# Diagonal score blocks of an HGRN2 recurrence as two alternating 64-column products

## The chip, the core and the metric

The kernel runs on one core of one Trainium2 chip. The metric is the device time of one execution in microseconds (us); lower is better. Three executions of the kernel before took 622.64, 622.67 and 622.85 us, a median of 622.67 us. Inputs and outputs are float32.

## The reference, cut to what matters

One decoder layer with model width 1024 over 512 tokens: a gated linear recurrence (HGRN2, 8 heads of 128) and a latent attention (8 heads) run side by side, are gated, merged, and added to the residual stream. The change concerns only the scores inside the recurrence. It is computed in chunks of 32 tokens:

```python
b = jnp.cumsum(log_f, axis=3)
q_in = q * jnp.exp(b)
k_in = k * jnp.exp(-b)
k_out = k * jnp.exp(b_last - b)
scores = jnp.einsum('nbhtk,nbhsk->nbhts', q_in, k_in)
scores = jnp.where(causal, scores, 0.0)
o_intra = jnp.einsum('nbhts,nbhsv->nbhtv', scores, v)
# between chunks: state = state * decay + k_out^T v ; o_inter = q_in . state
```

## The kernel before, in words

The kernel is one long stream of products on TensorE, fed by weights that arrive by DMA. Most products are the projections of the 512 tokens with the weight matrices. Each float32 weight is split on the chip into a high part (a ScalarE cast, line 113) and a low part (a VectorE subtraction, line 114), and a projection is three products (lines 90, 91 and 92, in helper `mm3`).

The recurrence is done for pairs of heads (`hg_pair`, called for pairs 0 to 2 in the loop at line 716 and for the last pair at line 733). A pair projects the forget gate and works out running products of it (`hg_forget`), projects values, queries and gate, builds the states at the ends of 128-token tiles (`hg_states`), and then computes scores (`hg_scores`), outputs (`hg_out`) and gated results (`hg_gate`). The kernel does not use chunks of 32 on their own: it joins four chunks into a tile of 128 tokens and carries a state only between tiles. So each head has NT = 4 diagonal score blocks of 128 keys by 128 queries, and the pairs of chunks inside such a block need differently scaled operands. `hg_scores` therefore writes a block in three layers, one over the other, into one PSUM tile `aps` per head:

- line 511: `ki` times `qi`, the whole 128x128 block. Right on the four 32x32 chunk diagonals; elsewhere it is written over or masked.
- line 517: `ko` times `qi`, 32x32 blocks for chunk 0 to chunk 1 (PSUM partitions 0 to 31) and chunk 2 to chunk 3 (partitions 64 to 95). Its loop runs over the two chunk positions outside and the four tiles inside.
- line 522: `k64` times `q64`, a 64x64 block for the first two chunks to the last two.

In the words of the change, products that start at PSUM partition 0 and products that start at partition 64 belong to different column groups of TensorE; a product's number of output partitions is its number of weight columns (the profile writes 128*32 for 128 rows and 32 columns). `C` is 32, `P` is 128. All three layers are plain float32 products, each of which shows in the trace as two weight loads and two matmuls: line 511 makes 16 matmuls for a pair of heads, line 517 makes 32, line 522 makes 16.

Line 523 is one VectorE instruction per head, a predicated copy: where `mask_le` (key not after query) is set, it copies the PSUM tile to `asb` in SBUF. `asb` is set to zero once at the start (line 434), so masked places stay zero. `hg_out` then multiplies `asb` with the values (line 533) and adds the part from the states (line 535); ScalarE squares the result (line 539), GpSimd works out the root of the mean (lines 160 and 161), VectorE scales (line 541), and TensorE turns the result around (line 549).

The order on each engine comes from the framework's planner, which simulates the program from its own costs (`schedule_with_timeline_sim=True`, line 1145), so for pairs 0 to 2 nobody has written out where the score products stand among the projections. For the last pair, TensorE's order is written out by hand (`manual_schedule`, line 726): scores, then a gate projection inside which the outputs are placed, then the first attention scores. PSUM tiles come from two pools: 3 banks for projections (`mm`) and 5 for everything else (`ax`).

Of the kernel before, what the change touches and what calls it, by code (L numbers as in the profile page):

```python
# [18 lines left out]
P = 128  # L19
D = 1024  # L20
S = 512
NT = S // P
# [16 lines left out]
def hybrid_layer(ctx: ExitStack, tc: tile.TileContext, a):  # L39
    nc = tc.nc  # L40
# [15 lines left out]
    def ax_tile():  # L56
        return ax.tile([P, 512], F32, tag="ax", name="ax_ps")
# [301 lines left out]
    mask_le = const.tile([P, P], U8, name="mask_le")  # L359
# [70 lines left out]
    for i in range(2):  # L430
        gh = hw.tile([P, NT, 12], F32, f"gh{i}")
        nc.gpsimd.memset(gh[:], 1.0)
        asb = hw.tile([P, S], F32, f"asb{i}")
# [71 lines left out]
    def hg_scores(heads):  # L505

        res = [(asb_[h % 2], ax_tile()) + t for h, t in heads]
        for _, aps, ki, ko, k64, qi, q64 in res:
            for i in range(NT):
                b = slice(i * P, i * P + P)  # L510
                nc.tensor.matmul(aps[:, b], ki[:, b], qi[:, b], start=True, stop=True)  # L511

        for _, aps, ki, ko, k64, qi, q64 in res:
            for c in (0, 2):
                for i in range(NT):
                    blk = lambda n: slice(i * P + n * C, i * P + n * C + C)
                    nc.tensor.matmul(aps[c * C : c * C + C, blk(c + 1)], ko[:, blk(c)], qi[:, blk(c + 1)],
                                     start=True, stop=True)
        for asb, aps, ki, ko, k64, qi, q64 in res:
            for i in range(NT):  # L520
                b = slice(i * 64, i * 64 + 64)
                nc.tensor.matmul(aps[0:64, i * P + 64 : i * P + P], k64[:, b], q64[:, b], start=True, stop=True)
            nc.vector.copy_predicated(asb[:].rearrange("p (g t) -> p g t", g=NT),
                                      mask_le[:].rearrange("p (o t) -> p o t", o=1).broadcast_to([P, NT, P]),
                                      aps[:].rearrange("p (g t) -> p g t", g=NT))
        return [r[0] for r in res]

    def hg_out(h, asb, st_, q128, v_sb):
# [30 lines left out]
    def hg_pair(pair, before_gate=None, last=None):  # L559
# [23 lines left out]
        def scores():  # L583
            return hg_scores([(h, kk[i][2:5] + qq[i][0:2]) for i, h in enumerate(hs)])
# [121 lines left out]
    def gates(b, c, hook=None, to=None):  # L706

        res = []
        for i, ps in enumerate(proj_ch(w_in, COL_G + b * D + c * 256, hT, hook)):
            j = 8 * b + 2 * c + i  # L710
            g = z_tile()[:] if to is None else to[:, 2 * c + i]
            nc.scalar.activation(g, ps[:], AF.Tanh, scale=0.5, bias=hb_gate[:, j : j + 1])
            res.append(g)
        return res
# [130 lines left out]
    g = first_gates  # L845
    for c in range(1, 4):
        g = g + gates(0, c, to=ma)
# [41 lines left out]
    part = {}  # L889
# [259 lines left out]
```

## Time and profile before

| | |
|---|---|
| median of three executions | 622.67 us |
| span of the profiled execution (first to last instruction) | 620.6 us |
| TensorE busy (PE) | 610.0 us, 98% |
| weight loads (PEld) | 521.3 us, 84% |
| VectorE busy (DVE) | 397.4 us, 64% |
| ScalarE busy (ACT) | 260.2 us, 42% |
| GpSimd busy (POOL) | 117.9 us, 19% |
| matmuls of line 511 / 517 / 522 | 64 / 128 / 64 |

The span runs from the first to the last instruction. The profile gives no separate total for the profiled execution; the 2.07 us between its span and the median lie outside the instructions. A matmul's duration in the trace covers its way through the array, and matmuls follow each other before the one ahead has ended; so a rate is read from the starts of neighbours, not from durations.

### The profile page before, as it was taken

The numbers are of one execution on the slowest core, as the hardware profiler recorded it, in microseconds if no ns is written. First come the engines' busy times: TensorE is split into PE (matmuls) and PEld (weight loads), VectorE is DVE, ScalarE is ACT, GpSimd is POOL, SyncE is SP. The second block draws the span as 40 slices with busy tenths as digits, with TensorE's granted clock in tenths as the row PEclk, the third lists the DMA queues.
The fourth block names the chain that finished last, engine by engine and source line by source line (L and its number), as shares of the span: only waits on it lengthen the run. The fifth ranks groups of instructions, "written<-read, shape, count | busy, mean of one in ns | idle before, by whom it ended". The sixth has DMA issues, their size and how long they took to land.

```text
span 620.6 us, 8808 instructions
## 1 busy us (share of the span) xinstructions
PE 610.0 (98%) x3336; PEld 521.3 (84%) x3336; DVE 397.4 (64%) x625; ACT 260.2 (42%) x483; POOL 117.9 (19%) x219
## 2 busy tenths in 40 slices
PE   8999999999999999999999999999999999999995
PEld 4998888888888888888888888888899988888884
DVE  7727855398864539847667767738257842447895
ACT  5645243323144231445445555444354532334352
POOL 3106300231320033231414123001210012000011
PEclk9999999999999999999999999999999999999998
DMA  7425153223205202423223232329942899600403
GB/s 248 143 67 175 63 145 92 69 69 101 69 2 170 80 22 56 118 53 106 74 70 101 56 87 85 101 69 326 248 123 56 268 356 288 200 0 1 169 1 135
DMA packets 62377, 72.35 MB, mean 117 GB/s; under 512 B 6104, under 2 KB 48510, under 8 KB 62336
## 3 DMA queue, kind: packets, MB, share of 16 engines
q1 hardware_dynamic: 58476, 61.37, 31.9%
q0 software_dynamic: 2160, 7.87, 6.3%
q10 hardware_dynamic: 1700, 2.56, 1.4%
q8 instruction: 26, 0.43, 0.3%
q14 instruction: 15, 0.12, 0.1%
HBM read 60.25 MB, written 2.10 MB: 100 GB/s over the span
## 4 chain that ended last, share of the span: by engine, by line
PE 96%; DVE 2%; ACT 1%; DMA 0%; issue 0%; POOL 0%; POOLq 0%; ACTq 0%; DVEq 0%
PE mm_ps L90 23%; PE mm_ps L92 23%; PE mm_ps L91 23%; PE ax_ps L875 6%; PE ax_ps L983 4%; PE ax_ps L672 2%; PE mm_ps L266 2%; PE ax_ps L693 1%; PE ax_ps L511 1%; PE ax_ps L533 1%; PE ax_ps L92 1%; PE ax_ps L91 1%; PE ax_ps L90 1%; PE mm_ps L875 1%; PE mm_ps L983 1%; PE ax_ps L535 1%
## 5 line engine op out<-in xcount | busy, mean ns | idle before, releaser
L114 DVE TENSOR_TENSOR w_lo<-w_raw,w_hi 128x1024 fp32r<-128x1024 f32 (+3 forms) x86 | 102.5, 1195 | 97.4 <-ACT w_hi L113 96.5
L90 PE MATMUL mm_ps<-hT,w_hi 128*128 128x512 f32 x384 | 150.9, 393 | 0.0
L91 PE MATMUL mm_ps<-hT,w_hi 128*128 128x512 f32 x384 | 150.0, 391 | 0.0
L92 PE MATMUL mm_ps<-hT,w_lo 128*128 128x512 f32 x384 | 149.8, 392 | 0.0
L113 ACT CAST w_hi<-w_raw 128x1024 fp32r<-128x1024 f32 (+3 forms) x86 | 85.1, 992 | 143.6 <-PE mm_ps L91 83.9
L92 PEld LDWEIGHTS mm_ps<-hT,w_lo 128*128 128x128 f32 x384 | 72.1, 188 | 14.6
L91 PEld LDWEIGHTS mm_ps<-hT,w_hi 128*128 128x128 f32 x384 | 72.2, 188 | 14.4
L90 PEld LDWEIGHTS mm_ps<-hT,w_hi 128*128 128x128 f32 x384 | 72.2, 188 | 14.3
L92 PE MATMUL mm_ps<-w_hi,hT 128*128 128x512 f32 (+1 forms) x96 | 36.7, 384 | 0.0
L91 PE MATMUL mm_ps<-w_lo,hT 128*128 128x512 f32 (+1 forms) x96 | 36.5, 382 | 0.0
L90 PE MATMUL mm_ps<-w_hi,hT 128*128 128x512 f32 (+1 forms) x96 | 36.4, 386 | 0.0
L680 POOL TENSOR_SCALAR p<-p,sm 128x128 f32<-128x128 f32 (+3 forms) x28 | 16.9, 606 | 64.1 <-DVE sm L679 37.8
L455 DVE RECIPROCAL tf<-pr 128x512 f32<-128x512 f32 x8 | 26.8, 3351 | 0.2
L678 ACT ACTIVATE p<-ax_ps,sm 128x128 f32<-128x128 f32 (+3 forms) x32 | 16.9, 530 | 23.6 <-DVE sm L677 21.1
L90 PE MATMUL mm_ps<-yb,w_hi 128*128 128x512 f32 x64 | 24.9, 389 | 0.0
L91 PE MATMUL mm_ps<-yb,w_hi 128*128 128x512 f32 x64 | 24.9, 389 | 0.0
L92 PE MATMUL mm_ps<-yb,w_lo 128*128 128x512 f32 x64 | 24.9, 389 | 0.0
L541 DVE TENSOR_TENSOR k<-ax_ps,ss 128x512 f32<-128x512 f32 x8 | 5.5, 692 | 24.7 <-POOL ss L161 24.7
L156 DVE TENSOR_TENSOR pt<-ax_ps,pt 128x512 fp32r<-128x512 f32 (+1 forms) x24 | 13.6, 593 | 11.3 <-ACT pt L155 11.3
L90 PE MATMUL mm_ps<-cT,w_hi 128*128 128x512 f32 x52 | 20.8, 400 | 0.0
L92 PEld LDWEIGHTS mm_ps<-w_hi,hT 128*128 128x128 f32 x96 | 18.0, 188 | 3.0
L91 PEld LDWEIGHTS mm_ps<-w_lo,hT 128*128 128x128 f32 x96 | 18.0, 188 | 2.9
(284 smaller groups left out, 1172.8 us busy)
## 6 DMA issues: line engine op xcount, KB each, us to landing
w_raw<-w_in SPq DMA_DIRECT2D x58, 512.0 KB, 3.8
x<-w_proj_a SPq DMA_DIRECT2D x10, 512.0 KB, 6.5
x<-x POOLq DMA_DIRECT2D x8, 512.0 KB, 9.6
w_raw<-w_proj_b SPq DMA_DIRECT2D x8, 512.0 KB, 9.3
w_raw<-w_proj_a SPq DMA_DIRECT2D x4, 512.0 KB, 11.4
ya<-w_out SPq DMA_DIRECT2D x4, 512.0 KB, 7.4
t<-w_out SPq DMA_DIRECT2D x4, 512.0 KB
yb<-w_out SPq DMA_DIRECT2D x4, 512.0 KB, 9.5
```

Source lines behind the costliest of these rows:

```text
L90: nc.tensor.matmul(ps, lh[lsl], rh[rsl], start=start, stop=False)
L91: nc.tensor.matmul(ps, lh[lsl], rl[rsl], start=False, stop=False)
L92: nc.tensor.matmul(ps, ll[lsl], rh[rsl], start=False, stop=stop)
L113: nc.scalar.copy(hi[:, :o], raw[:, :o])
L114: (lo_eng or nc.vector).tensor_tensor(lo[:, :o], raw[:, :o], hi[:, :o].bitcast(F32), op=ALU.subtract)
L156: nc.vector.tensor_tensor(lo, src, hi.bitcast(F32), op=ALU.subtract)
L266: nc.tensor.matmul(ps, hT[l][:, 4 * kh + k, t * P : t * P + P], c_hl[kh][r][:, k * 256 : k * 256 + 256], start=kh == 0 and kind == 0 and k ...
L455: nc.vector.reciprocal(rp[:], pr[:])
L678: nc.scalar.activation(p[:, :n], sps[:, :n], AF.Exp, scale=SCALE, bias=sm[:, 1:2], accum_out=sm[:, 2:3])
L680: (nc.vector if final else nc.gpsimd).tensor_scalar(p[:, :n], p[:, :n], sm[:, 3:4], 0.5, op0=ALU.mult, op1=ALU.mult)
L875: nc.tensor.matmul(ps[:, o], w[k // 2][i][:, k % 2, cols], ap[j][:, k], start=not banks and c == 0 and n == 0, stop=n == 11, skip_group_ch ...
L983: nc.tensor.matmul(ps[:, o : o + n], ap[i][:, k, t * P : t * P + P], w[k // 2][j][:, k % 2, o : o + n], start=fresh and c == 0, stop=c == ...
```

## The change

Three edits, all in `hg_scores`. The 128x128 product becomes two products of 64 keys by 64 queries, one at PSUM partitions 0 to 63 (columns 0 to 63 of the block) and one at partitions 64 to 127 (columns 64 to 127), alternating. The loops around the 32-column products are exchanged, so that the two column groups alternate with each product. The lower left 64x64 quarter of the block is no longer written, so the predicated copy becomes two: partitions 0 to 63 with all 128 columns of each tile, partitions 64 to 127 with the last 64.

```diff
             for i in range(NT):
-                b = slice(i * P, i * P + P)
-                nc.tensor.matmul(aps[:, b], ki[:, b], qi[:, b], start=True, stop=True)
+                for n in range(2):
+                    b = slice(i * P + n * 64, i * P + n * 64 + 64)
+                    nc.tensor.matmul(aps[n * 64 : n * 64 + 64, b], ki[:, b], qi[:, b], start=True, stop=True)
 
         for _, aps, ki, ko, k64, qi, q64 in res:
-            for c in (0, 2):
-                for i in range(NT):
+            for i in range(NT):
+                for c in (0, 2):
                     blk = lambda n: slice(i * P + n * C, i * P + n * C + C)
...
-            nc.vector.copy_predicated(asb[:].rearrange("p (g t) -> p g t", g=NT),
-                                      mask_le[:].rearrange("p (o t) -> p o t", o=1).broadcast_to([P, NT, P]),
-                                      aps[:].rearrange("p (g t) -> p g t", g=NT))
+            for n in range(2):
+                part, cols = slice(n * 64, n * 64 + 64), slice(n * 64, P)
+                view = lambda t: t[part].rearrange("p (g t) -> p g t", g=NT)[:, :, cols]
+                nc.vector.copy_predicated(view(asb), mask_le[part, cols].rearrange("p (o t) -> p o t", o=1)
+                                          .broadcast_to([64, NT, P - n * 64]), view(aps))
```

## The prediction

> **What bounds the kernel now.** I read the spans and clock first, then the windows, then the timeline around the scores.
>
> ```profile
> core 0: 620.6 us, clock 0.996
> ```
> ```profile
> core 0: us, PE busy (x) PEld busy (x) DVE busy (x) ACT busy (x) POOL busy (x), PEclk, DMA share, GB/s
> 0.00:18.00 18.00, 14.84 (x80) 9.27 (x80) 13.65 (x28) 9.73 (x19) 6.84 (x19) 1.00 0.80 269
> 18.00:613.20 595.20, 595.13 (x3257) 512.03 (x3257) 381.94 (x593) 248.62 (x460) 109.63 (x198) 1.00 0.39 112
> 613.20:620.60 7.40, 0.00 (x0) 0.00 (x0) 1.80 (x4) 1.85 (x4) 1.44 (x4) 0.63 0.37 142
> ```
>
> The middle row decides: from 18 us to TensorE's last matmul at about 613.2 us, TensorE has a matmul in flight for 595.13 of 595.20 us, at full clock. Nothing keeps it waiting long enough to empty it. A busy TensorE can still be a slow one, so the question is how densely its matmuls follow each other inside the scores. The chain of waits agrees on whose time counts:
>
> ```profile
> PE 96%; DVE 2%; ACT 1%; DMA 0%; issue 0%; POOL 0%; POOLq 0%; ACTq 0%; DVEq 0%
> ```
>
> So time taken off TensorE's stream comes off the end, as long as no other engine then makes TensorE wait. The scores of one pair of heads, in the timeline of TensorE (start, us from first start to last end, line, shape, count):
>
> ```profile
> 105.39 0.39 PE L92 MATMUL mm_ps<-hT,w_lo 128*128 128x512 f32 x1
> 105.62 1.95 PE L511 MATMUL ax_ps<-qi,ki 128*128 128x128 f32 x16
> 107.50 0.90 PE L517 MATMUL ax_ps<-qi,ko 128*32 128x32 f32 x32
> 108.33 1.15 PE L522 MATMUL ax_ps<-q,k 128*64 128x64 f32 x16
> 109.40 0.50 PE L90 MATMUL mm_ps<-hT,w_hi 128*128 128x512 f32 x1
> 109.74 0.39 PE L91 MATMUL mm_ps<-hT,w_hi 128*128 128x512 f32 x1
> ```
>
> The kernel has four such stages, one for each pair: 64 matmuls of line 511 are 4 x 16.
>
> ```profile
> L511 PE MATMUL ax_ps<-qi,ki 128*128 128x128 f32 x64 | 7.8, 275 | 0.0
> L517 PE MATMUL ax_ps<-qi,ko 128*32 128x32 f32 x128 | 3.6, 199 | 0.0
> L522 PE MATMUL ax_ps<-q,k 128*64 128x64 f32 x64 | 4.6, 225 | 0.0
> ```
>
> **How fast each width runs.** A narrower window of the timeline leaves out the first matmuls of a run:
>
> ```profile
> 105.73 1.84 PE L511 MATMUL ax_ps<-qi,ki 128*128 128x128 f32 x15
> 108.49 0.98 PE L522 MATMUL ax_ps<-q,k 128*64 128x64 f32 x14
> ```
>
> Taking off the last one's own duration: (1.84 - 0.275) / 14 = 112 ns from one 128-column matmul to the next, and (0.98 - 0.225) / 13 = 58 ns for 64 columns. Half the width, half the time, with 4 to 5 ns that stay; the line through both gives 31 ns for 32 columns. If 64-column products came strictly one after another, twice as many of them would gain nothing: 2 x 58 = 116 against 112. All hangs on whether two column groups run at once.
>
> Line 517 shows that they can. Its 32 matmuls take (0.90 - 0.199) / 31 = 22.6 ns each, below the 31 ns of one after another, though its loop changes the column group only three times in a stage. Windows on line 517 show where:
>
> ```profile
> 107.49:107.65 0.16, 0.15 (x5) 0.15 (x6) 1.00 0.00 0
> 107.80:107.95 0.15, 0.15 (x17) 0.15 (x12) 1.00 0.00 0
> ```
>
> A window counts what begins in it and what is still in flight. In the first 0.16 us there is one group alone and 5 matmuls. In the later window 17 are seen; one group alone, at 31 ns with 199 ns in flight, would show (150 + 199) / 31 = 11. So near a change of group the next group's matmuls start while the last ones of the group before are still waiting their turn: two streams side by side. The count comes to (150 + 199) / 17 = 20.5 ns per matmul.
>
> **The change, part by part.** *The diagonal blocks.* A stage now has 32 matmuls of 64 columns, two (one product) for one half, two for the other. If the halves run side by side, each half takes 16 x 58 = 0.93 us. I add 0.03 us for the second half's later start (half a step, an estimate). Changing the width costs something: the last matmul of line 511 starts at 105.73 + 14 x 0.112 = 107.30, its turn is over at 107.41, and line 517 starts at 107.50, 0.09 us later. Of line 522, the first two steps take 108.49 - 108.33 = 0.16 us instead of 2 x 0.058 = 0.12, another 0.04 to 0.05. Before, line 511 had the same width as the projections ahead of it and paid neither; now it pays 0.14 us. From its first turn to the start of line 517: before 107.50 - 105.62 = 1.88 us; after 0.14 + 0.93 + 0.03 + 0.09 = 1.19 us. That is -0.69 us a stage. If the halves don't overlap at all, it is 0.14 + 32 x 0.058 + 0.09 = 2.09, or +0.21 us. These are the ends; I take the overlap, since the nearest row, line 517, shows it for the same data type, operand rows and PSUM tile.
>
> *The 32-column products.* Before, 108.33 - 107.50 = 0.83 us, of which 0.09 is the change of width after them and about 0.02 the slow first step. With groups alternating throughout: 16 x 0.031 + 0.02 + 0.02 + 0.09 = 0.63 us, or -0.20. If the 20.5 ns counted above is all that can be issued, 32 x 0.0205 + 0.11 = 0.77, or -0.06. I take -0.15.
>
> *Line 522 and what follows it* stay as they are, the 0.11 us (109.74 - 109.40 against 0.23 of a usual projection step) that the return to full width costs included.
>
> *The predicated copy.* One instruction per head becomes two. Half the partitions is no cheaper, as line 626 shows beside line 523; half the elements is:
>
> ```profile
> L523 DVE COPY_PREDICATED asb<-mask_le,ax_ps 128x512 f32<-128x512 uint8 x8 | 5.4, 728 | 1.2 <-PE ax_ps L522 1.2
> L626 DVE TENSOR_TENSOR qp<-qs,qh 64x512 fp32r<-64x512 f32 x8 | 5.8, 721 | 5.1 <-ACT qh L622 4.9
> L156 DVE TENSOR_TENSOR pt<-ax_ps,pt 128x256 fp32r<-128x256 f32 x8 | 3.3, 414 | 0.0
> ```
>
> So 0.73 us plus about 0.42 (between half of 0.73 and 0.46), 0.42 us more for each head, 0.84 us for each stage, 3.4 us over the kernel, all on VectorE. What hides it is the projection work that TensorE does between the scores and the outputs. In the stage where VectorE is most crowded:
>
> ```profile
> 164.82 1.35 DVE L523 COPY_PREDICATED asb<-mask_le,ax_ps 128x512 f32<-128x512 uint8 x2
> 169.71 0.60 PE L533 MATMUL ax_ps<-v,asb 128*128 128x128 f32 x4
> ```
>
> The copies end at 166.17 and TensorE wants `asb` at 169.71, 3.54 us later. If VectorE ends 0.84 us later and TensorE comes 0.84 us earlier, 1.9 us are left. Queued behind the copies on VectorE are the forget gates' steps and weight splits of the next pair; 0.84 us is little against the 381.94 busy of 595.20 us above.
>
> What is late next is the turn of the outputs, line 549, which needs VectorE's line 541:
>
> ```profile
> 122.00 0.69 DVE L541 TENSOR_TENSOR k<-ax_ps,ss 128x512 f32<-128x512 f32 x1 [1.19 <-POOL ss L161]
> 123.33 0.60 PE L549 MATMUL ax_ps<-ident,k 128*128 128x128 f32 x4
> ```
>
> Here only 123.33 - 122.69 = 0.64 us are spare. But that chain (squares, root, scaling) begins with TensorE's own outputs, so it moves ahead with TensorE; it would hurt only as far as it stands still, at worst 0.84 - 0.64 = 0.2 us in a stage, which I keep as the end of the range and take as nothing.
>
> *Sum.* -0.69 - 0.15 = -0.84 us a stage, x 4 = -3.4 us. The span goes from 620.6 to 617.2; outside it lie 622.67 - 620.6 = 2.07 us that the edit doesn't touch. Forecast: 622.67 - 3.4 = 619.3 us. Ends for this case: at most -1.0 a stage (no late start, cheap changes of width), 618.6; at least -0.75 a stage with 0.2 given back, 4 x 0.55 = 2.2, 620.5.
>
> **Where the Trainium skill speaks against it.** "TensorE: Matmul & The Clock Gate", Part 3, section "The mechanism", says that a weight load runs beside earlier matmuls only if its row group differs, and that matmuls start and end strictly in program order. All products here use all 128 rows, so by that rule alternating columns would gain nothing. Line 517 disagrees at 32 columns (17 matmuls where 11 would fit). "TensorEngine Tiling (Array Packing)", section "Key Properties", says instead that different tiles load and multiply in parallel, 128x64 having two; no run here yet shows it at 64.
>
> **Rivals.** *No overlap at 64 columns* (the change doesn't do what it says for the larger part): +0.21 from line 511 and -0.15 from line 517 make +0.06 us a stage, +0.2 us in all: 622.9 us, no change that can be measured. For it: the only 64-column rows in the profile, line 522, use a single column group. Against it: line 517. If line 517 loses its gain too, it is 4 x 0.21 = 0.84 us, 623.5 us, still within what can't be told. Chance of both 0.08. The first page's rule, taken at its word, ends at 623.5 us.
>
> *Half an overlap*, where loads share a path: two halves at 44 instead of 29 ns per matmul cost 32 x 0.015 = 0.48 us a stage more than forecast; 621.2 us. Chance 0.06.
>
> *Each change of column group costs what a change of width costs*, 0.09 us. Line 511 would make 15 such changes in a stage and line 517 15 instead of 3. With the serial +0.21, that is 0.21 + 27 x 0.09 = 2.6 us a stage, 10.6 us, 633.3 us: clearly slower. The point from which it decides lies at (0.31 - 0.21) / 27 = 4 ns per change, above which the result is slower by over 1.25 us. Against it: line 517's changes of group are where it is fastest. Chance 0.02.
>
> *The planner sets another order* for pairs 0 to 2, because its costs changed, and TensorE gets a wait or some more changes of width at 0.09 to 0.11 us. Nothing in the profile speaks for it except that the order there isn't written out. It would take twelve of them to eat 1.2 us; 620.0 to 623. Chance 0.04.
>
> **How the numbers follow.** A measurement of this kernel can tell about 0.2%, 1.25 us, from no change, so faster means below 621.4 and slower above 623.9. The forecast has 0.80. Faster: 0.80, most of the half overlap and a part of the planner, 0.86. Same: no overlap and the rest, 0.11. Slower: 0.03. The range reaches from 618.4, a little under the forecast's own lower end, to 621.2, which takes in the half overlap; no overlap and changes that cost stay out.
>
> **What would show it.** Right: line 511 (its new line) with 128 matmuls of 64 columns, 32 of them in a stage in about (0.14 + 0.96) us plus a duration of 0.22; line 517's 32 in about 0.7 us from first start to last end; line 523 with 16 instructions, two forms, about 0.73 and 0.42 us; TensorE still busy without a break from 18 us to its last matmul, which ends near 609.8 us. Wrong: 64-column matmuls of that line 58 ns apart on average (no overlap); a row of waits of TensorE for `asb` or for line 541; projections with another order ahead of the scores.

## The result and the profile after

The changed kernel takes 619.08 us (median of five executions, 618.88 to 619.32) against 622.67 us before (622.48 to 622.85). The ratio is 0.9943, with a 95% interval from 0.9931 to 0.9955: 3.6 us, 0.6%, faster.

The windows of the changed kernel, with the same columns as before (the end of TensorE's work has moved to 610.1 us):

```profile
18.00:610.10 592.10, 592.00 (x3323) 508.66 (x3321) 385.03 (x601) 248.93 (x460) 109.76 (x198) 1.00 0.39 112
610.10:617.60 7.50, 0.00 (x0) 0.00 (x0) 1.80 (x4) 1.85 (x4) 1.47 (x4) 0.72 0.36 140
```

TensorE still has a matmul in flight for all but 0.1 us of the stretch. It does 66 more matmuls in it (64 from the change, two at the window's edges), in 3.1 us less. VectorE works 3.1 us more. The last window, behind TensorE, is about as long as before (7.50 and 7.40 us). So the time came out of TensorE's stream, and the timeline of the first score stage shows where:

```profile
105.54 0.39 PE L92 MATMUL mm_ps<-hT,w_lo 128*128 128x512 f32 x1
105.86 1.15 PE L512 MATMUL ax_ps<-qi,ki 128*64 128x64 f32 x32
106.94 0.70 PE L518 MATMUL ax_ps<-qi,ko 128*32 128x32 f32 x32
107.57 1.15 PE L523 MATMUL ax_ps<-q,k 128*64 128x64 f32 x16
108.64 0.50 PE L90 MATMUL mm_ps<-hT,w_hi 128*128 128x512 f32 x1
108.98 0.39 PE L91 MATMUL mm_ps<-hT,w_hi 128*128 128x512 f32 x1
```

Read from the last projection ahead of the scores to the second one behind them, this is 108.98 - 105.54 = 3.44 us, against 109.74 - 105.39 = 4.35 us before. The first stage lost 0.91 us. The other three, read the same way from the matmul ahead of the scores, lost 0.91 us each as well (4.23 to 3.33 us). Four times 0.91 makes 3.64 us, and 3.59 were measured. The 32 matmuls of the new halves take as long from first start to last end (1.15 us) as the 16 equally wide ones of line 523 below them. That is what two streams side by side look like.

The copies became two kinds, one as dear as before, one cheaper:

```profile
L527 DVE COPY_PREDICATED asb<-mask_le,ax_ps 64x512 f32<-64x512 uint8 x8 | 5.8, 728 | 0.1
...
L527 DVE COPY_PREDICATED asb<-mask_le,ax_ps 64x256 f32<-64x256 uint8 x8 | 3.6, 451 | 0.1
```

### The profile page after: what moved, and what is told of

Its sections match the earlier page's. It is cut to its first block, busy times and chain, and to the rows that moved or that the text cites. A ratio compares the mean times of both kernels' runs of the same rounds, so it can differ in the third digit from the quotient of the medians.

```text
span 617.6 us, 8947 instructions
## 1 busy us (share of the span) xinstructions
PE 607.3 (98%) x3400; PEld 518.2 (84%) x3400; DVE 400.5 (65%) x633; ACT 260.4 (42%) x483; POOL 117.9 (19%) x219
## 4 chain that ended last, share of the span: by engine, by line
PE 96%; DVE 2%; ACT 1%; DMA 0%; issue 0%; POOL 0%; POOLq 0%; ACTq 0%; DVEq 0%
PE mm_ps L90 23%; PE mm_ps L91 23%; PE mm_ps L92 23%; PE ax_ps L878 6%; PE ax_ps L986 4%; PE ax_ps L675 2%; PE mm_ps L266 2%; PE ax_ps L696 1%; PE ax_ps L536 1%; PE ax_ps L92 1%; PE ax_ps L91 1%; PE ax_ps L90 1%; PE mm_ps L878 1%; PE mm_ps L986 1%; PE ax_ps L538 1%; PE ax_ps L498 1%
## 5 line engine op out<-in xcount | busy, mean ns | idle before, releaser
L92 PEld LDWEIGHTS mm_ps<-w_hi,hT 128*128 128x128 f32 x96 | 18.0, 188 | 3.0
L90 PEld LDWEIGHTS mm_ps<-w_hi,hT 128*128 128x128 f32 x96 | 18.0, 188 | 3.0
L92 PE MATMUL mm_ps<-cT,w_lo 128*128 128x512 f32 x52 | 20.3, 390 | 0.0
```

The lines of the kernel that those rows point to most:

```text
L90: nc.tensor.matmul(ps, lh[lsl], rh[rsl], start=start, stop=False)
L92: nc.tensor.matmul(ps, ll[lsl], rh[rsl], start=False, stop=stop)
```

## The experiments

The theory is that of the prediction: matmuls in two column groups run side by side, and TensorE's stream is the time of the kernel. The rivals are that narrower products are cheaper by themselves, that another order by the planner brought the gain, and that the copies take part in it. Unless said otherwise a time is a median of several executions, and the kernel before took 622.69 us (first four runs) and 622.66 us (the others) beside them.

**The blocks alone**

```diff
-            for i in range(NT):
-                for c in (0, 2):
+            for c in (0, 2):
+                for i in range(NT):
                     blk = lambda n: slice(i * P + n * C, i * P + n * C + C)
```

(Against the changed kernel, like the diffs below.)

> The changed kernel with the 32-column products back in their old order (position outside, tile inside); the 64-column halves and the two copies stay. Theory (two column groups run side by side, and what leaves TensorE's stream leaves the end): the blocks alone are worth 0.71 us in each of four stages, 2.8 us, so about 619.9 us, 0.8 us above the changed kernel. Rival (the whole gain comes from another order that the planner found, so the parts don't add up): anything, for instance no gain at all, 622.7 us.

Measured: 620.14 us, ratio 0.9965 (0.9953 to 0.9978), 2.55 us below the kernel before.

**The loop alone**

The same exchange of loops, made in the kernel before, with nothing else.

> The kernel before with the two loops around the 32-column products exchanged and nothing else. Theory: 32 matmuls from 0.83 to 0.63 us up to the next product in each stage, 4 x 0.20 = 0.8 us, about 621.9 us; together with the run that has the blocks alone it makes up the 3.6 us of the whole change. Rival (20.5 ns a matmul was already the rate of issue): 4 x 0.06 = 0.2 us, 622.4 us.

Measured: 621.84 us, ratio 0.9987 (0.9978 to 0.9996), 0.85 us below. In the timeline of its first stage, the 32 matmuls stand closer and all else is as before:

```profile
105.66 1.95 PE L511 MATMUL ax_ps<-qi,ki 128*128 128x128 f32 x16
107.53 0.70 PE L517 MATMUL ax_ps<-qi,ko 128*32 128x32 f32 x32
108.16 1.15 PE L522 MATMUL ax_ps<-q,k 128*64 128x64 f32 x16
```

The spacing is (0.70 - 0.197) / 31 = 16 ns, half of the 31 ns of one group, so 20.5 ns was no limit of issue. 2.55 + 0.85 = 3.4 us: the parts add up to the whole within what these runs can tell. The traces also set the planner's order aside. Told apart by source line, tile and shape, the instructions of TensorE, VectorE, ScalarE and GpSimd stand in the same order in this run as in the kernel before, and in the same order in the blocks alone as in the changed kernel, but for the exchanged products themselves. So the 0.85 us here, and the 1.06 us between the blocks alone and the changed kernel, can't come from another order.

**The halves in turn**

```diff
-        for _, aps, ki, ko, k64, qi, q64 in res:
-            for i in range(NT):
-                for n in range(2):
+        for n in range(2):
+            for _, aps, ki, ko, k64, qi, q64 in res:
+                for i in range(NT):
                     b = slice(i * P + n * 64, i * P + n * 64 + 64)
```

> The changed kernel with its 64-column products in another order: first all first halves of both heads, then all second halves, so that the column group changes once in a stage and not with each product. Work, widths, copies and everything else as in the changed kernel. Theory: two runs of 16 matmuls at 58 ns, 1.87 us, less some 0.17 us of overlap where the group changes, against 0.94 us: 0.76 us more a stage, about 622.1 us, nearly all of the gain gone. Rival (narrower products are cheaper by themselves, or the gain comes from the rest of the change): as the changed kernel, 619.1 us.

Measured: 622.31 us, ratio to the kernel before 0.9995 (0.9987 to 1.0004). Same products, same widths, same copies, same 32-column loop as the changed kernel; only the order of the halves differs, and 3.2 of the 3.6 us are gone. The timeline of the first stage:

```profile
105.52 1.90 PE L512 MATMUL ax_ps<-qi,ki 128*64 128x64 f32 x32
107.34 0.70 PE L518 MATMUL ax_ps<-qi,ko 128*32 128x32 f32 x32
```

1.90 us where alternation took 1.15. This rejects the rival that narrower products are cheaper by themselves. It rejects the planner too: all instructions outside the halves stand in the same order in both traces, on all four engines.

**The copies alone**

The two predicated copies of the changed kernel in the kernel before.

> The kernel before with only its predicated copy made into two; all products as before. Theory: VectorE works 8 x 0.45 = 3.6 us more and TensorE has 3.5 us of projections between scores and outputs, so nothing changes, 622.7 us. Rival (the copies delay the outputs or the next pair's steps on VectorE, and the change would be worth more without them): up to 0.9 us in each of four stages, 626.2 us at most.

Measured: 622.61 us, ratio 1.0 (0.9991 to 1.0009). Its windows show VectorE working 3.3 us more than before and TensorE as full as before:

```profile
18.00:613.20 595.20, 595.17 (x3257) 512.49 (x3257) 385.28 (x601) 248.89 (x460) 107.24 (x198) 1.00 0.38 111
```

The copies are hidden. In this run the planner did set another order of TensorE's other matmuls: 618 of 3080 places hold a matmul of another line, tile or shape than before. The time did not change with it.

**How many may stand in a row.** Two runs, each a single execution with its profile, change the column group after two products (four matmuls) or four products (eight):

```diff
-            for i in range(NT):
+            for i0 in range(0, NT, 2):
                 for n in range(2):
...
+                    for i in range(i0, i0 + 2):
...
```

(The first run; the second has 4 in place of both 2s in the added lines. The body of the loop, left out here, is the same, one step further in.)

> The changed kernel with its 64-column halves changing the column group after two products (four matmuls) instead of after each. Read in the first score stage, which takes 1.15 us there in the changed kernel. Theory (a matmul of the other column group can pass those that wait, but only some three of them, as line 517 of the kernel before showed, where the next group began with the fifth matmul of eight): four in a row are passed almost fully, so 1.15 to 1.25 us for the stage's 32 matmuls and about 619.2 us. Rival (order doesn't matter within a stage, or only strict alternation overlaps): 1.15 or 2.0 us.

> The same with a change after four products (eight matmuls), so three changes in a stage, the pattern that line 517 had before. Theory: the next group starts with the fifth of eight, so three periods of 5 x 58 ns and a last run of 8 x 58 ns, with 0.05 for the first step and 0.22 for the last duration: 0.87 + 0.41 + 0.05 + 0.22 = 1.55 us from first start to last end, and 4 x 0.4 = 1.6 us more than the changed kernel, 620.7 us. Rivals as for the run before: 1.15 or 2.0 us.

The first stage of each, in this order:

```profile
105.61 1.20 PE L513 MATMUL ax_ps<-qi,ki 128*64 128x64 f32 x32
```
```profile
105.65 1.54 PE L513 MATMUL ax_ps<-qi,ki 128*64 128x64 f32 x32
```

Expected were 1.15 to 1.25 and 1.55 us. The executions took 618.99 and 621.47 us, where about 619.2 and 620.7 were expected. The 0.8 us that the second is late lie outside its instructions: its span is 618.6 us, 2.9 us short of its time, while the five executions of the changed kernel have spans of 617.0 to 617.6 us, 1.7 to 2.2 us short of theirs.

The starts of single matmuls in the traces show the rule that carried the expectation. With eight in a row, and with sixteen (the halves in turn), the first matmul of the next group starts 5 to 7 ns behind the fourth-last of the row. So it passes three that wait, and no more. In the halves in turn these two starts are at 106.263 and 106.269 us, and nearly nothing is left of the overlap; in line 517 of the kernel before, two such starts are at 107.645 and 107.651 us.

**What a change of width costs**

The late 64x64 products move up to the other 64-column ones, ahead of the 32-column loop, so a stage changes width three times instead of four:

```diff
+        for _, aps, ki, ko, k64, qi, q64 in res:
+            for i in range(NT):
+                b = slice(i * 64, i * 64 + 64)
+                nc.tensor.matmul(aps[0:64, i * P + 64 : i * P + P], k64[:, b], q64[:, b], start=True, stop=True)
 
         for _, aps, ki, ko, k64, qi, q64 in res:
...
         for asb, aps, ki, ko, k64, qi, q64 in res:
-            for i in range(NT):
-                b = slice(i * 64, i * 64 + 64)
-                nc.tensor.matmul(aps[0:64, i * P + 64 : i * P + P], k64[:, b], q64[:, b], start=True, stop=True)
             for n in range(2):
```

> The changed kernel with the late 64x64 products (k64 times q64) moved up behind the 64-column halves, ahead of the 32-column products, so that a stage goes through widths 128, 64, 32, 128 instead of 128, 64, 32, 64, 128. Theory (a change of width costs time of its own): one change less, 0.09 to 0.14 us a stage, 0.4 to 0.6 us, about 618.6 us. Rival (the pause at a change of width is only the end of what was in flight and comes out the same elsewhere): 619.1 us. The copies then wait for both heads' products, which is 0.3 us later for the first head and should stay hidden.

Measured: 618.41 us, ratio 0.9935 (0.9923 to 0.9948), 0.67 us below the changed kernel's median, 0.17 us a stage. The times of the two kernels overlap (618.17 to 619.13 and 618.88 to 619.32 us), but their spans do not (616.4 to 616.6 and 617.0 to 617.6 us). Its timeline:

```profile
105.38 0.39 PE L92 MATMUL mm_ps<-hT,w_lo 128*128 128x512 f32 x1
105.70 1.15 PE L512 MATMUL ax_ps<-qi,ki 128*64 128x64 f32 x32
106.68 1.10 PE L516 MATMUL ax_ps<-q,k 128*64 128x64 f32 x16
107.70 0.70 PE L522 MATMUL ax_ps<-qi,ko 128*32 128x32 f32 x32
108.33 0.50 PE L90 MATMUL mm_ps<-hT,w_hi 128*128 128x512 f32 x1
108.67 0.40 PE L91 MATMUL mm_ps<-hT,w_hi 128*128 128x512 f32 x1
```

From line 92 to the second projection behind, 108.67 - 105.38 = 3.29 us against 3.44: 0.15 us, about the 0.09 us of waiting and the 0.05 us of a slow first step.

**Weights or queries**

Each late 64x64 product is cut into two of 32 keys by 64 queries, in two column groups:

```diff
             for i in range(NT):
-                b = slice(i * 64, i * 64 + 64)
-                nc.tensor.matmul(aps[0:64, i * P + 64 : i * P + P], k64[:, b], q64[:, b], start=True, stop=True)
+                for n in range(2):
+                    b, bk = slice(i * 64, i * 64 + 64), slice(i * 64 + n * 32, i * 64 + n * 32 + 32)
+                    nc.tensor.matmul(aps[n * 32 : n * 32 + 32, i * P + 64 : i * P + P], k64[:, bk], q64[:, b],
+                                     start=True, stop=True)
```

> The changed kernel with each late 64x64 product cut into two of 32 keys by 64 queries, in two column groups in alternation. If the weight columns set the 58 ns of a 64-column matmul, each group takes 16 x 31 ns = 0.5 us instead of 0.93 for the whole, and the change of width ahead of them goes too: 0.5 us a stage, 2 us in all, 617.1 us. If the 64 queries that are streamed set it, each group takes 16 x 58 ns, 0.93 us as now, and only the change of width is saved: 0.1 us a stage, 618.6 us.

Measured: 618.23 us, ratio 0.9929 (0.9916 to 0.9943), nearer to the second case. The timeline says more:

```profile
106.83 0.58 PE L518 MATMUL ax_ps<-qi,ko 128*32 128x32 f32 x25
107.21 0.24 PE L524 MATMUL ax_ps<-q,k 128*32 128x64 f32 x1
107.21 0.23 PE L518 MATMUL ax_ps<-qi,ko 128*32 128x32 f32 x3
107.27 1.06 PE L524 MATMUL ax_ps<-q,k 128*32 128x64 f32 x31
```

31 matmuls in two groups stand (1.06 - 0.22) / 30 = 28 ns apart. By itself this could also be one stream at 28 ns, near the 31 ns that the weight columns would give. But the single starts are not evenly spaced: gaps of 19 to 20 ns and of 36 to 37 ns take turns, which is two streams of 56 ns beside each other, near the 58 ns of 64 weight columns. The last run below shows both lengths in one line: early in the stage, matmuls of 32 keys by 32 queries in one group start 32 ns apart, and those of 32 keys by 64 queries 56 ns apart. For these float32 products it is the 64 columns that are streamed that take the time, and halving the weights gives nothing by itself. The gain, 0.85 us, is put down to the saved change of width and some overlap with the products ahead: the first matmul of line 524 starts before the last three of line 518, which precede it in the program.

**Four column groups, and everything 32 wide**

The diagonal blocks as four products of 32 keys. Chunks 1 and 3 are multiplied with the 64 queries of their half, so that all that the copies read has been written:

```diff
             for i in range(NT):
-                for n in range(2):
-                    b = slice(i * P + n * 64, i * P + n * 64 + 64)
-                    nc.tensor.matmul(aps[n * 64 : n * 64 + 64, b], ki[:, b], qi[:, b], start=True, stop=True)
+                for n in range(4):
+                    b = slice(i * P + n * C, i * P + n * C + C)
+                    q = slice(i * P + n // 2 * 64, i * P + n * C + C)
+                    nc.tensor.matmul(aps[n * C : n * C + C, q], ki[:, b], qi[:, q], start=True, stop=True)
```

> The changed kernel with the diagonal blocks as four products of 32 keys (32 or 64 queries) in four column groups in turn, instead of two of 64; the rest as changed. Theory (groups are independent, as many as there are): each group has 16 matmuls, at 31 ns for 32 queries and at 31 to 58 ns for 64, 0.5 to 0.93 us against 0.94, and the change of width after them goes: 0.1 to 0.55 us a stage, 616.9 to 618.7 us. Rival (no more than two matmuls can be started in 29 to 31 ns, so 64 matmuls take 64 x 15 to 20 ns = 1.0 to 1.3 us): 0 to 0.3 us a stage worse, 619 to 620.3 us.

> The two runs before this one together: all score products 32 columns wide, so that a stage changes width only on its way in and out. Theory: the gains of both add, and one more change of width is saved where two of them met: between 616 and 618.5 us. Rival (the rate of issue bounds it): 128 matmuls a stage at 15 to 20 ns are 1.9 to 2.6 us against 2.6 us of the three products as changed, 616.5 to 619.1 us.

Measured: 617.69 us for the four groups, ratio 0.9925 (0.9913 to 0.9938), and 616.75 us with the late products cut as well, ratio 0.9907 (0.9894 to 0.9921). The first lies outside the range of its rival. The second lies in both ranges, so its timeline has to decide. It beats both kernels: 5.9 us below the one before, 2.3 us below the changed one. In its first stage the start of the diagonal blocks reads:

```profile
105.25 0.39 PE L92 MATMUL mm_ps<-hT,w_lo 128*128 128x512 f32 x1
105.57 0.93 PE L513 MATMUL ax_ps<-qi,ki 128*32 128x32 f32 x57
106.29 0.22 PE L519 MATMUL ax_ps<-qi,ko 128*32 128x32 f32 x1
```

57 matmuls, some with 32 queries and some with 64, start within 0.72 us or so, 13 ns apart. Two groups alone would take at least 31 / 2 = 15.5 ns each, so more than two groups do run at once, and starting two matmuls in 29 to 31 ns is no limit. The one matmul of line 519 in the last row starts ahead of the seven of line 513 that are left, six of which have 64 queries and so belong to two column groups. So three is not the most that can be passed in all. Three for each column group would fit, but no run tests that. The next projections come at:

```profile
107.81 0.50 PE L90 MATMUL mm_ps<-hT,w_hi 128*128 128x512 f32 x1
108.14 0.39 PE L91 MATMUL mm_ps<-hT,w_hi 128*128 128x512 f32 x1
```

The stage takes 108.14 - 105.25 = 2.89 us instead of 3.44, 0.55 us less, 2.2 us for four.

## Why the prediction was right, point by point

**The bound.** TensorE's stream was taken for the time of the kernel. It was: 3.64 us less in the four stages, 3.59 us less at the end, and the copies on VectorE cost nothing when made alone.

**The diagonal blocks**, forecast at -0.69 us a stage: from line 92 to the start of the 32-column products it is 106.94 - 105.54 = 1.40 us, against 107.50 - 105.39 = 2.11 before, -0.71. The two streams fully overlap, (1.15 - 0.225) / 31 = 30 ns for each matmul. The cost of the added change of width is there: line 512 starts 0.32 us after line 92, where a projection step is 0.23. The 0.03 us kept for a late second half were not needed: its first matmul starts 6 ns behind the other's. The length named as a sign, 0.14 + 0.96 + 0.22 = 1.32 us for the 32 matmuls, was too long against 1.15: besides those 0.03 us, 0.09 us of it lie ahead of the first start, and the last matmul is counted with both its step of 0.06 and its duration. The halves in turn show that this term hangs on the alternation, as argued.

**The 32-column products**, forecast at -0.15 between -0.06 and -0.20: 107.57 - 106.94 = 0.63 us against 0.83, -0.20, the full overlap. The lower end rested on taking the 20.5 ns counted in a window of line 517 for a rate of issue. It was the mean of a stretch that overlaps in part only.

**Line 522 and the return to full width** were to stay: 108.98 - 107.57 = 1.41 us, as 109.74 - 108.33 = 1.41 before.

**The copies**: 0.73 and 0.45 us, forecast 0.73 and 0.42. In the crowded second stage 1.9 us were to be left between them and the outputs. The last copy on VectorE and the first product on TensorE that reads `asb`:

```profile
166.14 0.45 DVE L527 COPY_PREDICATED asb<-mask_le,ax_ps 64x256 f32<-64x256 uint8 x1
```
```profile
168.06 0.49 PE L536 MATMUL ax_ps<-v,asb 128*128 128x128 f32 x3
```

That is 168.06 - 166.59 = 1.47 us. Other VectorE steps stand between the copies of the two heads, but the cover held.

**The sum**, 3.4 us, fell short of the measured 3.59 mostly by the 32-column term. TensorE's last matmul, expected to end near 609.8 us, ended near 610.1. That execution is the slowest of the five (a span of 617.6 us, the others 617.0 to 617.2), and in it the last projection ahead of the first score stage already began 0.15 us later than before (105.54 against 105.39), ahead of any changed instruction.

**The planner** was a rival with a chance of 0.04, and its sign, another order of the projections, did appear: of the 3080 matmuls outside the scores, 569 places in TensorE's order hold another one than before, from about 114 us on. It cost nothing that the traces show. Up to the start of the last matmul, what lies outside the four score stages takes 595.8 us before, and 595.8 to 596.4 us in the seven programs that share the new order; the 596.4 is that of the changed kernel's execution just named.

**The rule that spoke against it.** The Trainium skill, "TensorE: Matmul & The Clock Gate", Part 3, "The mechanism", lets a weight load run beside matmuls only where row groups differ and has matmuls start in program order. Here all products use all 128 rows and two column groups ran at twice the rate of one, and a matmul of line 524 started ahead of three that stand before it in the program. The measurement decides. That the rule leaves nothing to gain from columns was the prediction's own inference. The statement of the Trainium skill in "TensorEngine Tiling (Array Packing)", "Key Properties", that tiles load and multiply in parallel, agrees with the traces: 30 ns a matmul at 64 columns, 16 at 32.

## What to carry to other kernels

When TensorE is always busy, compare the spacing of its matmuls with that of other widths before believing that it is full: two streams of narrow products in different column groups took as long here as one. Alternate the group with every product or two, not after a long run, and keep products of one width together, since each change of width cost 0.11 to 0.15 us here. Pay for it on an engine with room, and check that the room is there in the most crowded place, not on average.

## What the runs showed of the hardware that was not expected

The time of a narrow float32 matmul followed the columns that were streamed, not the weight columns: 32 weights by 64 queries took 56 ns in a group, like 64 by 64 with 58, and 32 by 32 took 32. Four column groups went further than two, with 57 matmuls started 13 ns apart. And with two column groups the overlap reached only three matmuls past those that wait in the other group, which the single starts show, and the stage times for groups changed after 2, 4, 8 and 16 matmuls: 1.15, 1.20, 1.54 and 1.90 us.
